# Zero rows in the first block's keys, and 32 bytes more in front of the phase pools

## The chip, the cores and the metric

One core of one Trainium2 chip runs the whole program in one launch. The metric is the device time of one execution in microseconds (us); less is better. The kernel before takes 3259.42 us, the median of three runs (3257.91 to 3260.88 us).

## The reference

Two different transformer blocks, two layers each, run one after the other on 512 tokens of width 1024, in float32. The change touches the attention of the first block and, by the places of tiles in memory, every phase of both. Cut to that:

```python
def differential_attention(q, k, v, lam_full, subln_g, lambda_init):
    s = jnp.einsum('bqhcd,bkhcd->bhcqk', qblk, kk) * Dh ** -0.5     # Dh = 64, two maps c per head
    p = jax.nn.softmax(s, axis=-1)
    a = p[:, :, 0] - lam_full * p[:, :, 1]
    return jnp.einsum('bhqk,bkhe->bqhe', a, v)

def dilated_window_attention(q, k, v, dilation, n_side):            # three dilations, 8 heads of 64
    s = jnp.einsum('brnqhd,brnkhd->brnhqk', qb, kn) * (Dh ** -0.5)
    s = jnp.where(mask, s, NEG_INF)
    e = jnp.exp(s - jnp.max(s, axis=-1, keepdims=True))
    o = jnp.einsum('brnhqk,brnkhd->brnqhd', e, vn) / den

def swiglu(h, w_gate_up, w_down):
    g, u = jnp.split(h @ w_gate_up, 2, axis=-1)
    return (jax.nn.silu(g) * u) @ w_down
```

## The kernel before, in words

**Matmuls.** Nearly every product is made of float32r matmuls on split operands: a float32 value is kept as a high part and a low part, and `mm3` (lines 309 to 313) adds high by high, and the two mixed products, in one PSUM bank: three matmuls of 128 rows, 128 weight columns and 512 (in some places 256, 360 or 384) moving columns for each step of 128 in the contraction.

**Weights.** `weights` hands them out in the order of a written plan. The SP queue loads each chunk of 1 MB, ScalarE makes the high part (line 255), VectorE the low part (line 257). The tiles `wh`, `wl` lie in the pool `stage`, the transposed activations `hTh`, `hTl` in the pool `base`. For a few chunks next to a change of phase, `spare` places `wh`, `wl` in the pool of the phase instead.

**Pools.** `setup` opens `const`, `stage`, `base` and `small`, and each phase opens its own pool behind them. `small` holds 15 tiles of 32 bytes (line 345). So the first tile of a phase pool starts 480 bytes behind the start of `small`, and an odd number of small tiles of 32 bytes shifts what follows by half a line of 64 bytes.

**Mixer of the first block** (`mixer1`). A unit (`unit`, `unit_rest`, lines 520 to 559) projects the q and k of two heads, or of one head with its two maps: for each of the two chunks c, 24 matmuls into a bank `upsum`, then the rotation: VectorE shuffles and multiplies, GpSimd (POOL) multiplies and adds. For a split unit ScalarE and VectorE then build the stack `st`: in its planes 0 and 1 the q of head e (or map e), high in its own 64 rows and low in the other 64, in planes 2 and 3 the high part of k in both halves of the rows, in plane 4 the low part of k, the rows 0 to 63 for e = 0 and 64 to 127 for e = 1. A plain unit (`d1`, `d2`) keeps q and k in float32 in two planes.

**Scores.** `score2` (lines 610 to 615) needs two matmuls: one over all 128 rows (line 613), high k against high and low q, and one over the 64 rows of e (line 615), low k against high q. Differential attention (`da_items`) does it for two maps in each of 4 blocks of 128 queries for each of 4 heads. The dilated attention (`dil_items`) does it once in each of 4 blocks for each of 8 heads, and then makes one 128-column float32 score for each of the other two dilations, over the 64 rows of its head (line 697); such a matmul shows as two passes in the trace. `weave` mixes the steps of these attentions with the units of the next heads, so that scores, transposes (lines 650, 720), value products and projections alternate on TensorE. The framework that records the program sets the final order on each engine and the waits.

**Other phases.** `merge1` makes the gates (48 matmuls a step, `gates`), the products `ab` from the tiles `oabh`, `oabl`, and the output product `acc` from `mgh`, `mgl`. `ffn1` and `ffn2` make `gu` from `hTh`, `hTl` (weights stationary) and the down product `acc` from `acth`, `actl` (weights moving). `merge2` makes its `acc` like `merge1`. At the turn of a phase, where the transposes of the next activations come in pieces, the first units (`ufirst`) and the first `gu` are made in two halves of 256 columns.

Of the kernel before, what the change touches and what calls it, by code (L numbers as in the profile page):

```python
# [224 lines left out]
class Kern:  # L225
# [118 lines left out]
    def sm(self, n, name):  # L344
        return self.small.tile([128, 8], F32, tag="sm", name=name, bufs=15)[:, :n]

# [188 lines left out]
    def unit_rest(self, c, ps, st, scale):  # L535

        nc = self.nc
        C, Sn = self.rope[:, 0, :], self.rope[:, 1, :]
        plain = st.shape[1] == 2
        sh = self.mix.tile([128, 512], F32, tag="rsh", name="rsh", bufs=2)  # L540
        z = st[:, c, :] if plain else self.mix.tile([128, 512], F32, tag="rz", name="rz", bufs=2)
        nc.vector.stream_shuffle(sh, ps, _SHUF)  # L542
        nc.vector.tensor_tensor(z, ps, C, op=OP.mult)
        nc.gpsimd.tensor_tensor(sh, sh, Sn, op=OP.mult)  # L544
        nc.gpsimd.tensor_tensor(z, z, sh, op=OP.add)
        if plain:
            return
        if c == 0:
            nc.scalar.activation(st[0:64, 0, :], z[0:64], AF.Copy, scale=scale)
            nc.scalar.activation(st[64:128, 1, :], z[64:128], AF.Copy, scale=scale)  # L550
            nc.vector.scalar_tensor_tensor(st[64:128, 0, :], z[0:64], scale, st[0:64, 0, :].bitcast(F32), op0=OP.mult, op1=OP.subtract)
            nc.vector.scalar_tensor_tensor(st[0:64, 1, :], z[64:128], scale, st[64:128, 1, :].bitcast(F32), op0=OP.mult, op1=OP.subtract)
        else:
            nc.scalar.activation(st[0:64, 2, :], z[0:64], AF.Copy)
            nc.scalar.activation(st[64:128, 3, :], z[64:128], AF.Copy)
            nc.scalar.activation(st[64:128, 2, :], z[0:64], AF.Copy)
            nc.scalar.activation(st[0:64, 3, :], z[64:128], AF.Copy)
            nc.vector.tensor_tensor(st[0:64, 4, :], z[0:64], st[0:64, 2, :].bitcast(F32), op=OP.subtract)
            nc.vector.tensor_tensor(st[64:128, 4, :], z[64:128], st[64:128, 3, :].bitcast(F32), op=OP.subtract)

    def stk(self, name):
        return self.mix.tile([128, 5, 512], F32R, tag="stk", name=name, bufs=3)

    def zst(self, name):
        return self.mix.tile([128, 2, 512], F32, tag="zst", name=name, bufs=4)

    def vfirst(self, keys, V):

        acc = [self.ps1(t, "vfirst") for t in "ssto"]
        for half, key in enumerate(keys):  # L570
            w = self.weights(key, 4, 512)
            for r in range(4):
                for k in range(4):
                    l = tuple(t[:, 4 * half + k, 128 * r:128 * r + 128] for t in self.hT)
                    self.mm3(acc[r], l, tuple(t[:, k, :] for t in w), half == 0 and k == 0, half == 1 and k == 3)
        lo = [self.mix.tile([128, 2, 512], F32R, tag="zst", name="Vl", bufs=4) for _ in range(2)]
        for r in range(4):
# [32 lines left out]
    def score2(self, out, st, e, q, k):  # L610

        mm = self.nc.tensor.matmul
        mm(out, st[:, e, q], st[:, 2 + e, k], start=True, stop=False)
        h = slice(64 * e, 64 * e + 64)
        mm(out, st[h, e, q], st[h, 4, k], start=False, stop=True)

    def da_items(self, h, st, V, Vl):
# [36 lines left out]
        def s4(rp):  # L654
# [7 lines left out]
            if rp == 1:  # L662
                nc.scalar.activation(self.oab[:, 0, h, :], O, AF.Copy)
                sq = self.mix.tile([128, 512], F32, tag="rz", name="dasq", bufs=2)
                nc.scalar.activation(sq, O, AF.Square)
# [21 lines left out]
    def dil_items(self, j, e, sts, V):  # L687
# [3 lines left out]
        def s1(r):  # L691
            ps = self.ps2("dis")
            q = slice(128 * r, 128 * r + 128)
            self.score2(ps[0], sts[0], e, q, slice(0, 512))
            own = slice(64 * e, 64 * e + 64)
            for g in (1, 2):
                nc.tensor.matmul(ps[1][:, 128 * g - 128:128 * g], sts[g][own, 0, q], sts[g][own, 1, q], start=True, stop=True)
            P = self.mix.tile([128, 1024], F32, tag="P", name="diP", bufs=3)
# [72 lines left out]
    def mixer1(self, l):  # L771
        nc, tc, aps = self.nc, self.tc, self.aps
        with tc.tile_pool(name=f"mix{l}", bufs=1, reuse_waits="tile") as mix:
# [9 lines left out]

            lam = mix.tile([128, 4, 64], F32, tag="rz", name="lam", bufs=2)
            la = aps["lam"]
# [6 lines left out]
            nc.scalar.activation(ls, ls, AF.Exp)  # L792
            self.nlam = mix.tile([128, 1], F32, name="nlam")
            nc.vector.tensor_tensor(self.nlam, ls[:, 1:2], ls[:, 0:1], op=OP.subtract)
# [13 lines left out]
            def pair_units(j):  # L808

                d = [None, self.zst("d1"), self.zst("d2")]  # L810
                Vj = []

                def first():
# [3 lines left out]
                def values():  # L817
                    Vj.append(self.newV(False))
                    yield from self.vprod([("vp", l, j, 0), ("vp", l, j, 1)], 384, Vj[0])
                return d, Vj, [self.unit(("dil", l, j, 1), d[1]), self.unit(("dil", l, j, 2), d[2]), first(), values()]  # L820

# [9 lines left out]
            d, Vj, gens = pair_units(0)  # L831
            for h, n in zip((2, 2, 3, 3), range(4)):
                fills[h].append(gens[n])
            for h in range(4):
                self.weave(chain(fills[h]), 18 * len(fills[h]), self.pipeline(self.da_items(h, sts[h], V, Vl), *STAGES_DA), 10)
            for j in range(4):
# [331 lines left out]
    def mixer2(self, l, early):  # L1168
        nc, tc, aps = self.nc, self.tc, self.aps
        with tc.tile_pool(name=f"mixb{l}", bufs=1, reuse_waits="tile") as mix:  # L1170
# [5 lines left out]
            cols = {}  # L1176
            for n, w in (("pool_scale_2", 2), ("mla_g_cq_2", 2), ("mla_g_ckv_2", 1)):
                cols[n] = mix.tile([128, w], F32, name="c_" + n)
                nc.scalar.dma_start(cols[n], aps[n + "_cols"][l])
# [430 lines left out]
```

## Time and profile before

| | us |
|---|---|
| median of three runs | 3259.42 |
| lowest, highest | 3257.91, 3260.88 |
| the profiled execution | 3256.16 |
| its span, first to last instruction | 3254.4 |
| TensorE (PE) busy in the span | 3198.2 |
| VectorE (DVE) busy | 1882.8 |
| ScalarE (ACT) busy | 1288.8 |
| GpSimd (POOL) busy | 320.2 |

The profiled execution took 1.8 us more than its span, and 3.3 us less than the median. Matmuls are pipelined: a matmul's duration holds the time in which its results drain, so the time that one costs is the distance from its start to the start of the next, and this is read from the starts in the timeline, or from the count of matmuls in a stretch in which PE is always busy.

### The profile page before, as it was taken

The numbers are of one execution on the slowest core, as the hardware profiler recorded it, in microseconds if no ns is written. First come the engines' busy times: TensorE is split into PE (matmuls) and PEld (weight loads), VectorE is DVE, ScalarE is ACT, GpSimd is POOL, SyncE is SP. The second block draws the span as 40 slices with busy tenths as digits, with TensorE's granted clock in tenths as the row PEclk, the third lists the DMA queues.
The fourth block names the chain that finished last, engine by engine and source line by source line (L and its number), as shares of the span: only waits on it lengthen the run. The fifth ranks groups of instructions, "written<-read, shape, count | busy, mean of one in ns | idle before, by whom it ended". The sixth has DMA issues, their size and how long they took to land.

```text
span 3254.4 us, 39464 instructions
## 1 busy us (share of the span) xinstructions
PE 3198.2 (98%) x15756; PEld 2613.1 (80%) x15756; DVE 1882.8 (58%) x3276; ACT 1288.8 (40%) x2268; POOL 320.2 (10%) x286
## 2 busy tenths in 40 slices
PE   8999999999999999999999999999999999999999
PEld 6788888888888788888888889668888896688887
DVE  6766666666326766666666426896332368853323
ACT  4544443433224444443422224664232246632222
POOL 1222200030001222200000000020000001200000
PEclk9999999999999999999999999999999999999999
DMA  4111124366323111124345323213223322132222
GB/s 152 46 59 59 65 100 172 132 226 223 120 102 130 37 67 59 59 99 167 137 175 199 130 92 135 67 44 136 91 91 117 121 93 72 46 128 100 94 98 84
DMA packets 62392, 351.83 MB, mean 108 GB/s; under 512 B 9276, under 2 KB 9660, under 8 KB 29184
## 3 DMA queue, kind: packets, MB, share of 16 engines
q1 hardware_dynamic: 52528, 324.59, 27.9%
q10 hardware_dynamic: 7920, 18.08, 1.7%
q0 software_dynamic: 1760, 6.65, 0.7%
q8 instruction: 123, 2.02, 0.3%
q14 instruction: 61, 0.50, 0.0%
HBM read 336.91 MB, written 12.38 MB: 107 GB/s over the span
## 4 chain that ended last, share of the span: by engine, by line
PE 92%; DVE 5%; ACT 1%; issue 0%; POOL 0%; DMA 0%; DVEq 0%; ACTq 0%; POOLq 0%
PE gu L311 10%; PE gu L313 10%; PE gu L312 10%; PE acc L311 7%; PE acc L313 7%; PE acc L312 7%; PE upsum L311 4%; PE upsum L312 3%; PE upsum L313 3%; PE gates L312 2%; PE gates L311 2%; PE gates L313 2%; DVE wl L257 2%; PE O L1425 1%; PE vacc L312 1%; PE vacc L311 1%
## 5 line engine op out<-in xcount | busy, mean ns | idle before, releaser
L257 DVE TENSOR_TENSOR wl<-wr,wh 128x1024 fp32r<-128x1024 f32 (+3 forms) x519 | 637.4, 1260 | 437.3 <-ACT wh L255 429.9
L255 ACT ACTIVATE wh<-wr 128x1024 fp32r<-128x1024 f32 (+3 forms) x520 | 492.9, 988 | 885.9 <-PE gu L312 386.9
L311 PE MATMUL gu<-hTh,wh 128*128 128x512 f32 (+1 forms) x1536 | 571.3, 372 | 0.0
L313 PE MATMUL gu<-hTh,wl 128*128 128x512 f32 (+1 forms) x1536 | 570.0, 371 | 0.0
L312 PE MATMUL gu<-hTl,wh 128*128 128x512 f32 (+1 forms) x1536 | 569.9, 371 | 0.0
L311 PEld LDWEIGHTS gu<-hTh,wh 128*128 128x128 f32 x1536 | 288.8, 188 | 54.3 <-ACT wh L255 3.4
L313 PEld LDWEIGHTS gu<-hTh,wl 128*128 128x128 f32 x1536 | 288.8, 188 | 49.9
L312 PEld LDWEIGHTS gu<-hTl,wh 128*128 128x128 f32 x1536 | 288.8, 188 | 49.8
L907 DVE TENSOR_TENSOR sg<-sg,gu 128x512 f32<-128x512 f32 x88 | 60.3, 687 | 460.0 <-PE gu L313 459.0
L311 PE MATMUL acc<-wh,acth 128*128 128x512 f32 x704 | 278.6, 396 | 0.0
L313 PE MATMUL acc<-wh,actl 128*128 128x512 f32 x704 | 277.9, 395 | 0.0
L312 PE MATMUL acc<-wl,acth 128*128 128x512 f32 x704 | 277.8, 395 | 0.0
L311 PE MATMUL upsum<-hTh,wh 128*128 128x512 f32 x448 | 188.6, 421 | 0.0
L312 PE MATMUL upsum<-hTl,wh 128*128 128x512 f32 x448 | 176.9, 395 | 0.0
L313 PE MATMUL upsum<-hTh,wl 128*128 128x512 f32 x448 | 176.4, 394 | 0.0
L544 POOL TENSOR_TENSOR rsh<-rsh,rope 128x512 f32<-128x512 f32 x64 | 87.5, 1367 | 746.7 <-DVE rsh L542 514.7
L313 PEld LDWEIGHTS acc<-wh,actl 128*128 128x128 f32 x704 | 132.0, 187 | 32.2
L312 PEld LDWEIGHTS acc<-wl,acth 128*128 128x128 f32 x704 | 132.0, 187 | 31.8
L311 PEld LDWEIGHTS acc<-wh,acth 128*128 128x128 f32 x704 | 132.0, 187 | 31.8
L906 ACT ACTIVATE sg<-gu 128x512 f32<-128x512 f32 x88 | 52.2, 598 | 262.8 <-PE gu L313 258.8
L294 DVE SCALAR_TENSOR_TENSOR m<-wr,ccols,m 128x512 f32<-128x512 f32 x168 | 126.6, 753 | 17.6 <-DMA wr<-in_wst_dram 13.2
L311 PEld LDWEIGHTS upsum<-hTh,wh 128*128 128x128 f32 x448 | 84.1, 188 | 27.6 <-issue 8.9
(419 smaller groups left out, 6076.9 us busy)
## 6 DMA issues: line engine op xcount, KB each, us to landing
wr<-in_wst_dram SPq DMA_DIRECT2D x258, 1024.0 KB, 4.8
wr<-in_wst_dram SPq DMA_DIRECT2D x28, 512.0 KB, 3.8
wr<-in_wst_dram SPq DMA_DIRECT2D x16, 768.0 KB, 4.2
xs<-x SPq DMA_DIRECT2D x12, 512.0 KB, 3.4
x<-xs SPq DMA_DIRECT2D x3, 2048.0 KB
bias<-toep SPq DMA_DIRECT2D x16, 256.0 KB, 3.7
toep<-frs POOLq DMA_DIRECT2D x12, 320.0 KB, 3.3
fu<-modrows ACTq DMA_DIRECT2D x6, 512.0 KB
```

Of the source, the lines that this page charges most:

```text
L255: self.nc.scalar.activation(hi[:, a:b], raw[:, a:b], AF.Copy)
L257: eng.tensor_tensor(lo[:, a:b], raw[:, a:b], hi[:, a:b].bitcast(F32), op=OP.subtract)
L294: nc.vector.scalar_tensor_tensor(macc, w, sc, macc, op0=OP.mult, op1=OP.add)
L311: mm(out, l[0], r[0], start=start, stop=False)
L312: mm(out, l[0], r[1], start=False, stop=False)
L313: mm(out, l[1], r[0], start=False, stop=stop)
L544: nc.gpsimd.tensor_tensor(sh, sh, Sn, op=OP.mult)
L906: nc.scalar.activation(sg[:, 0:512], ps[0], AF.Silu)
L907: nc.vector.tensor_tensor(sg[:, 512:1024], sg[:, 0:512], ps[1], op=OP.mult)
L1425: nc.tensor.matmul(O[0:64, 128 * i - 128 + a:128 * i + 128], lv, PT[:, kc, a:], start=kc == 0, stop=kc == i)
```

## The change

- The low part of k gets a plane for each e (planes 4 and 5), with zeros in the 64 rows of the other one, and the k of a plain unit gets two planes in the same way. The second matmul of `score2` and the float32 scores of the dilated attention then run over all 128 rows; what the zero rows add is zero.
- The zeros are two POOL memsets of 64 rows by 512 for every unit, ahead of the POOL work of its second chunk; the k of a plain unit is added in two POOL instructions of 64 rows instead of one of 128.
- `stk` grows to 6 planes and 4 buffers and also takes the `Vl` tiles and both plain units of a pair (`d12`); the rotation's working tile `z` alternates between one tile `rz` and a plane of `oab` that is written late (`scratch`).
- `small` has 16 tiles instead of 15; `nlam` is widened to 64 bytes and two small tiles of the second block's mixer are put into one, so that the tiles behind them stay where they were within a line.

The built programs place the operands of the float32r matmuls at these bytes of a 64-byte line:

| tiles | before | after |
|---|---|---|
| `wh`, `wl` in `stage`; `hTh`, `hTl` | 32 | 32 |
| stacks, values and `pth`, `ptl` of the mixers | 32 | 32 |
| `oabh`, `oabl`, `mgh`, `mgl`, `acth`, `actl` | 0 | 32 |
| `wh`, `wl` of the spare chunks in phase pools | 0 | 32 |

The diff, cut to its core:

```diff
@@ sm: the pool of small tiles
-        return self.small.tile([128, 8], F32, tag="sm", name=name, bufs=15)[:, :n]
+        return self.small.tile([128, 8], F32, tag="sm", name=name, bufs=16)[:, :n]
@@ unit_rest
-        plain = st.shape[1] == 2
+        plain = st.shape[1] == 3
+        halves = slice(0, 64), slice(64, 128)
         sh = self.mix.tile([128, 512], F32, tag="rsh", name="rsh", bufs=2)
-        z = st[:, c, :] if plain else self.mix.tile([128, 512], F32, tag="rz", name="rz", bufs=2)
+        z = st[:, 0, :] if plain and c == 0 else self.scratch()
         nc.vector.stream_shuffle(sh, ps, _SHUF)
         nc.vector.tensor_tensor(z, ps, C, op=OP.mult)
+        if c == 1:
+            for e in range(2):
+                other = (st[halves[1 - e], 1 + e, :] if plain else st[halves[1 - e], 4 + e, :].bitcast(F32))
+                nc.gpsimd.memset(other, 0.0)
         nc.gpsimd.tensor_tensor(sh, sh, Sn, op=OP.mult)
-        nc.gpsimd.tensor_tensor(z, z, sh, op=OP.add)
+        if plain and c == 1:
+            for e in range(2):
+                nc.gpsimd.tensor_tensor(st[halves[e], 1 + e, :], z[halves[e]], sh[halves[e]], op=OP.add)
+        else:
+            nc.gpsimd.tensor_tensor(z, z, sh, op=OP.add)
...
-            nc.vector.tensor_tensor(st[64:128, 4, :], z[64:128], st[64:128, 3, :].bitcast(F32), op=OP.subtract)
+            nc.vector.tensor_tensor(st[64:128, 5, :], z[64:128], st[64:128, 3, :].bitcast(F32), op=OP.subtract)
+    def scratch(self):
+        self.turn = 1 - self.turn
+        return self.oab[:, 1, 3, :] if self.turn else self.rz
     def stk(self, name):
-        return self.mix.tile([128, 5, 512], F32R, tag="stk", name=name, bufs=3)
+        return self.mix.tile([128, 6, 512], F32R, tag="stk", name=name, bufs=4)
     def zst(self, name):
-        return self.mix.tile([128, 2, 512], F32, tag="zst", name=name, bufs=4)
+        t = self.mix.tile([128, 6, 512], F32, tag="stk", name=name, bufs=4)
+        return t[:, 0:3, :], t[:, 3:6, :]
@@ vfirst
-        lo = [self.mix.tile([128, 2, 512], F32R, tag="zst", name="Vl", bufs=4) for _ in range(2)]
+        lo = self.mix.tile([128, 6, 512], F32R, tag="stk", name="Vl", bufs=4)
+        lo = lo[:, 0:2, :], lo[:, 2:4, :]
@@ score2
         mm(out, st[:, e, q], st[:, 2 + e, k], start=True, stop=False)
-        h = slice(64 * e, 64 * e + 64)
-        mm(out, st[h, e, q], st[h, 4, k], start=False, stop=True)
+        mm(out, st[:, e, q], st[:, 4 + e, k], start=False, stop=True)
@@ da_items, s4
-                sq = self.mix.tile([128, 512], F32, tag="rz", name="dasq", bufs=2)
+                sq = self.scratch()
@@ dil_items, s1
-            own = slice(64 * e, 64 * e + 64)
             for g in (1, 2):
-                nc.tensor.matmul(ps[1][:, 128 * g - 128:128 * g], sts[g][own, 0, q], sts[g][own, 1, q], start=True, stop=True)
+                nc.tensor.matmul(ps[1][:, 128 * g - 128:128 * g], sts[g][:, 0, q], sts[g][:, 1 + e, q], start=True, stop=True)
@@ mixer1
+            self.rz = mix.tile([128, 512], F32, name="rz")
...
-            self.nlam = mix.tile([128, 1], F32, name="nlam")
+            self.nlam = mix.tile([128, 16], F32, name="nlam")[:, 0:1]
...
-                d = [None, self.zst("d1"), self.zst("d2")]
+                d = [None, None, None]
+                def others():
+                    d[1:] = self.zst("d12")
+                    yield from self.unit(("dil", l, j, 1), d[1])
+                    yield from self.unit(("dil", l, j, 2), d[2])
@@ mixer2
+            two = mix.tile([128, 4], F32, name="c_two")
+            for n, w, at in (("pool_scale_2", 2, 0), ("mla_g_cq_2", 2, 2), ("mla_g_ckv_2", 1, None)):
+                cols[n] = mix.tile([128, w], F32, name="c_" + n) if at is None else two[:, at:at + w]
```

On POOL, in layer 0 around the first pair of plain units (in heads 2 and 3 of the differential attention; `rsh` is the shuffled copy, `d_607`, `d_608` and `d_1029` the k and q of the plain units, `d_1303` the stack of the split unit after them; waits name engines) there stood:

```order
L544 TENSOR_TENSOR rsh<-rsh,rope 128x512 [waits DVE_49]
L545 TENSOR_TENSOR d_607<-d_607,rsh 128x512 [waits DVE_49,Pool_49]
L544 TENSOR_TENSOR rsh<-rsh,rope 128x512 [waits DVE_49]
L545 TENSOR_TENSOR d_607<-d_607,rsh 128x512 [waits DVE_49,Pool_49]
L544 TENSOR_TENSOR rsh<-rsh,rope 128x512 [waits DVE_49]
L545 TENSOR_TENSOR d_608<-d_608,rsh 128x512 [waits DVE_49,Pool_49]
L544 TENSOR_TENSOR rsh<-rsh,rope 128x512 [waits DVE_49]
L545 TENSOR_TENSOR d_608<-d_608,rsh 128x512 [waits DVE_49,Pool_49]
```

and now stands:

```order
L550 TENSOR_TENSOR rsh<-rsh,rope 128x512 [waits DVE_49]
L555 TENSOR_TENSOR d_1029<-d_1029,rsh 128x512 [waits DVE_49,Pool_49]
L549 MEMSET d_1303 64x512 [waits PE_49,Pool_49]
L549 MEMSET d_1303 64x512
L550 TENSOR_TENSOR rsh<-rsh,rope 128x512 [waits DVE_49,Pool_49]
L553 TENSOR_TENSOR d_1029<-oab,rsh 64x512 [waits DVE_49,Pool_49]
L553 TENSOR_TENSOR d_1029<-oab,rsh 64x512
L550 TENSOR_TENSOR rsh<-rsh,rope 128x512 [waits DVE_49,Pool_49]
L555 TENSOR_TENSOR d_1029<-d_1029,rsh 128x512 [waits DVE_49,Pool_49]
```

The memsets of the stack `d_1303` have moved ahead of the work of the plain units, and wait for TensorE to have read the last of what lay in that buffer.

On PE, in layer 0 at the start of head 1 (`das` are the scores of the differential attention, `upsum` the projection of the next unit, `dass` the sums of squares of head 0) there stood:

```order
L613 MATMUL das_850<-da_432 128x512
L615 MATMUL das_850<-da_432 128x512
L311 MATMUL upsum<-hTh,wh_611 128x512
L312 MATMUL upsum<-hTl,wh_611 128x512
L313 MATMUL upsum<-hTh,wl_612 128x512
L311 MATMUL upsum<-hTh,wh_611 128x512
L668 MATMUL dass<-ones_85,dasq 128x1 x4
```

and now stands:

```order
L631 MATMUL das_846<-da_433 128x512
L632 MATMUL das_846<-da_433 128x512
L631 MATMUL das_847<-da_433 128x512
L632 MATMUL das_847<-da_433 128x512
L311 MATMUL upsum<-hTh,wh_609 128x512
L312 MATMUL upsum<-hTl,wh_609 128x512
L313 MATMUL upsum<-hTh,wl_610 128x512
L685 MATMUL dass<-ones_85,rz 128x1 x4
```

A block's two pairs of score matmuls, which stood apart here, now stand together; elsewhere the order of PE and DVE differs by a few places of this kind in heads 0 to 2, and in the dilated attention it is the same but for the names of tiles.

## Rows read from the trace of the kernel before

**Rows 1.** The page's busy time of TensorE: share of the span and instructions.

```profile
PE 3198.2 (98%) x15756; PEld 2613.1 (80%) x15756; DVE 1882.8 (58%) x3276; ACT 1288.8 (40%) x2268; POOL 320.2 (10%) x286
```

**Rows 2.** The page's chain that ended last, by engine.

```profile
PE 92%; DVE 5%; ACT 1%; issue 0%; POOL 0%; DMA 0%; DVEq 0%; ACTq 0%; POOLq 0%
```

**Rows 3.** Busy time by stretch: length, PE, PEld, DVE, ACT, POOL, granted clock, DMA share, GB/s.

```profile
91.00:116.00 25.00, 25.00 (x119) 18.04 (x120) 21.07 (x38) 14.46 (x30) 6.63 (x5) 1.00 0.13 43
116.00:142.00 26.00, 24.81 (x118) 18.35 (x117) 21.54 (x40) 13.06 (x27) 7.38 (x5) 1.00 0.18 59
230.00:300.00 70.00, 69.36 (x384) 58.50 (x384) 45.29 (x96) 28.75 (x54) 16.02 (x11) 1.00 0.19 68
```

**Rows 4.** What PE waited for: us in total, times, longest.

```profile
PE vacc L312 <- DVE wl L257: 5.8, 10, 0.6
...
PE dapt L650 <- DVE ptl L608: 3.0, 4, 1.2
```

**Rows 5.** Timeline of PE in layer 0, differential scores: start, duration, instruction.

```profile
67.51 0.39 PE L613 MATMUL das<-da 128*128 128x512 f32 x1
67.83 0.50 PE L615 MATMUL das<-da 64*128 64x512 f32 x1
...
69.10 0.50 PE L311 MATMUL upsum<-hTh,wh 128*128 128x512 f32 x1
69.44 0.40 PE L312 MATMUL upsum<-hTl,wh 128*128 128x512 f32 x1
```

**Rows 6.** Costliest PE groups by form, the 64-row scores: count, busy, mean.

```profile
L615 PE MATMUL das<-da 64*128 64x512 f32 x64 | 31.7, 496 | 0.0
L615 PE MATMUL dis<-d 64*128 64x512 f32 x64 | 31.7, 496 | 0.0
```

**Rows 7.** Timeline of PE in layer 0, dilated scores.

```profile
228.06 0.39 PE L613 MATMUL dis<-d 128*128 128x512 f32 x1
...
228.71 0.60 PE L697 MATMUL dis<-d 64*128 64x128 f32 x4
229.25 0.50 PE L311 MATMUL upsum<-hTh,wh 128*128 128x512 f32 x1
229.58 0.40 PE L312 MATMUL upsum<-hTl,wh 128*128 128x512 f32 x1
```

**Rows 8.** Timeline of PE, full-row float32 passes between float32r matmuls.

```profile
95.57 0.95 PE L668 MATMUL dass<-ones,dasq 128*128 128x1 f32 x8
...
96.70 0.39 PE L313 MATMUL upsum<-hTh,wl 128*128 128x512 f32 x1
```

**Rows 9.** PE alone by stretch: length, busy (matmuls), clock; gu, acc, vfirst.

```profile
2300.00:2400.00 100.00, 100.00 (x443) 1.00 0.28 103
...
885.00:965.00 80.00, 80.00 (x345) 1.00 0.28 100
...
1029.00:1047.00 18.00, 18.00 (x81) 1.00 0.01 4
```

**Rows 10.** PE groups by form whose operand moves in its line, line 311 alone.

```profile
L311 PE MATMUL acc<-wh,acth 128*128 128x512 f32 x704 | 278.6, 396 | 0.0
...
L311 PE MATMUL acc<-wh,mgh 128*128 128x512 f32 x256 | 102.0, 398 | 0.0
...
L311 PE MATMUL ab<-oabh,wh 128*128 128x512 f32 x128 | 50.7, 397 | 0.0
```

**Rows 11.** Timeline of PE: first gu of 256 columns, three starts 48 matmuls apart.

```profile
644.59 0.28 PE L311 MATMUL gu<-hTh,wh 128*128 128x256 f32 x1
...
650.33 0.28 PE L311 MATMUL gu<-hTh,wh 128*128 128x256 f32 x1
...
655.94 0.40 PE L311 MATMUL gu<-hTh,wh 128*128 128x512 f32 x1
```

**Rows 12.** POOL groups by form: adds of plain units, and a memset of 64 rows.

```profile
L545 POOL TENSOR_TENSOR d<-d,rsh 128x512 f32<-128x512 f32 x32 | 54.6, 1705 | 2.5
...
L1238 POOL MEMSET ck<- 64x1024 f32 x4 | 3.8, 947 | 839.5 <-PE acc L313 839.4
```

More of the change, by code (lines that the diff above doesn't have):

```diff
@@ L782, in mixer1 @@
             linit = 0.8 - 0.6 * math.exp(-0.3 * l)
-            lam = mix.tile([128, 4, 64], F32, tag="rz", name="lam", bufs=2)
+            self.rz = mix.tile([128, 512], F32, name="rz")
+            self.turn = 0
+            lam = mix.tile([128, 4, 64], F32, tag="rsh", name="lam", bufs=2)
             la = aps["lam"]
@@ L819, in values @@
                     yield from self.vprod([("vp", l, j, 0), ("vp", l, j, 1)], 384, Vj[0])
-                return d, Vj, [self.unit(("dil", l, j, 1), d[1]), self.unit(("dil", l, j, 2), d[2]), first(), values()]
+                return d, Vj, [others(), first(), values()]
             def chain(gs):
@@ L831, in mixer1 @@
             d, Vj, gens = pair_units(0)
-            for h, n in zip((2, 2, 3, 3), range(4)):
+            for h, n in zip((2, 3, 3), range(3)):
                 fills[h].append(gens[n])
             for h in range(4):
-                self.weave(chain(fills[h]), 18 * len(fills[h]), self.pipeline(self.da_items(h, sts[h], V, Vl), *STAGES_DA), 10)
+                self.weave(chain(fills[h]), 18 if h < 2 else 36, self.pipeline(self.da_items(h, sts[h], V, Vl), *STAGES_DA), 10)
             for j in range(4):
@@ L1176, in mixer2 @@
             cols = {}
-            for n, w in (("pool_scale_2", 2), ("mla_g_cq_2", 2), ("mla_g_ckv_2", 1)):
-                cols[n] = mix.tile([128, w], F32, name="c_" + n)
+            two = mix.tile([128, 4], F32, name="c_two")
+            for n, w, at in (("pool_scale_2", 2, 0), ("mla_g_cq_2", 2, 2), ("mla_g_ckv_2", 1, None)):
+                cols[n] = mix.tile([128, w], F32, name="c_" + n) if at is None else two[:, at:at + w]
                 nc.scalar.dma_start(cols[n], aps[n + "_cols"][l])
```

## The prediction

> **What bounds the kernel now.** I read the page's busy times first: TensorE (PE) is busy for 3198.2 of the 3254.4 us of the span [rows 1], and the chain of work that ended last runs over PE for 92% of the span [rows 2]. So a time that PE no longer needs comes off the end, as long as nothing else is late in that place. The view by stretch says where something could be: PE is never idle in head 1 of the differential attention (25.00 of 25.00 us), but VectorE (DVE) works there 21.07 us; in the dilated attention DVE has 45.29 of 70.00 us [rows 3]. The waits of PE are few: 5.8 us in ten waits of `vacc` for low parts of weights, 3.0 us in four waits of the transposes `dapt` for `ptl`, all made by DVE [rows 4]. The granted clock is 1.00 in each of these stretches, the upper level of 2.4 GHz [rows 3].
>
> A matmul's duration includes the drain, which overlaps the next, so I price by starts.
>
> **Scores of the differential attention.** The timeline shows a block's four scores and the projection behind them: from the first score at 67.51 us to the second `upsum` at 69.44 us, five matmuls take 1.93 us [rows 5]. Five matmuls of 512 columns in a run take between 5 x 226.8 and 5 x 233.2 ns (these spacings are worked out below from [rows 9]); I take 231, since a run that is broken by other work sits between. That is 1.16 us, so each block pays 0.77 us for going from 128 rows to 64 and back. Two of the 64 `das` matmuls at line 615 belong to a block [rows 6], which makes 32 blocks and 32 x 0.77 = 24.6 us. After the change all of them use 128 rows, and the cost goes.
>
> **Scores of the dilated attention.** Two score matmuls, four float32 passes over 64 rows and the next `upsum` go from 228.06 to 229.58 us: 1.52 us [rows 7]. With all rows used I price three matmuls at 231 ns, 0.69 us, and the passes from the nearest full-row float32 work: eight passes and one `upsum` take 95.57 to 96.70 us, 1.13 us, so a pass costs (1130 - 227) / 8 = 113 ns with the change of type there and back in it [rows 8]. Four make 0.45 us. The block saves 1.52 - 1.14 = 0.38 us, and there are 64 [rows 6]: 24.3 us. Scores together: 48.9 us. With 226.8 ns instead of 231 it would be 32 x 0.796 + 64 x 0.388 = 50.3 us; the other end is nothing, if what costs here is not the number of rows (third rival).
>
> The Trainium skill (TensorE: Matmul & The Clock Gate, Part 3, "What overlaps and what doesn't") says that a weight load overlaps a running matmul only when the row groups differ. By that rule all matmuls on 128 rows would wait for their weights after the change, and the scores would save nothing. The trace does not agree for full rows: `gu` needs new 128-row weights for every matmul and starts one every 226.8 ns [rows 9].
>
> **Placement.** The stretches of [rows 9] are filled with matmuls of the same shape at the same clock, and each count takes in two that were still running when the stretch began. `gu`, with both operands at byte 32 of their lines: 100.00 us / 441 = 226.8 ns. `acc` of the feed-forward, with its moving weights at 32 and its stationary activations at 0: 80.00 us / 343 = 233.2 ns. What else differs is that weights move in `acc`; in `vfirst` they move too, against `hTh` at 32, and the spacing is 18.00 us / 79 = 227.8 ns. So I put the difference down to the place in the line, between 5.4 and 6.4 ns a matmul, and take 6.0. Three lines of each group in [rows 10] make 3 x (704 + 256 + 128) = 3264 matmuls. Of these 336 use spare weights that already share the half of the line; I value them at half. That gives (2928 + 168) x 6.0 = 18.6 us, with ends at 2928 x 5.4 = 15.8 and 3264 x 6.4 = 20.9 us.
>
> There is a price in it. At a change of phase, 48 matmuls of 256 columns take 650.33 - 644.59 = 5.74 us with weights at 32, the next 48, with spare weights at 0, 655.94 - 650.33 = 5.61 us [rows 11]: shared halves are 2.7 ns slower at this width. In seven such turns 96 matmuls each move to the shared half: 672 x 2.7 ns = +1.8 us. The transposes and the rest of the second block's mixer keep their places or are not paced by them: nothing.
>
> The Trainium skill (SBUF — State Buffer, "Who interferes with whom") gives PE two independent read ports and says that PE never waits on anyone; by it, the half of a line could not matter, and this term would be 0. The 226.8 against 233.2 ns of [rows 9] speak against that, unless the spacing comes from the role of the operand.
>
> **What is late next.** In head 1 PE's 25.0 us shrink by 4 x 0.77 = 3.1 to 21.9 us, and DVE needs 21.07 us of that [rows 3]. With DVE at 96%, the scores wait now and then for `danm`, and the transposes for `ptl`. In head 2 PE already stood for 1.2 of 26 us with DVE at 21.54 us [rows 3]. For heads 0 to 2 in both layers I take 0.8 us each, +4.8 us; the ends are 0 and 6 x 3.1 = 18.6 us, all that these heads saved. In the dilated attention DVE rises from 65% to about 68%; the ten waits of `vacc` may grow by 0.1 us each, +1.0 us.
>
> **POOL.** 64 memsets at half of the 947 ns of one twice as wide make 30 us; 16 second adds at 1705 ns at most make 27 us [rows 12]. POOL had 16.02 us of work in 70 [rows 3], and the q and k of a unit are made a whole pair, or two heads, ahead: this hides them. The memsets that moved ahead in POOL's order hold eight instructions of the plain units behind them until head 2's last score is read. What those make is first read after head 3, over 40 us later, so I cost it at nothing. DVE, ACT and DMA get no more work.
>
> **Sum.** -48.9 - 18.6 + 1.8 + 4.8 + 1.0 = -59.9 us. The profiled execution took 3256.16 us, so the same execution would take 3196.3. The median of the runs is 3.3 us above it, 3259.42; carried over, I predict 3199.5 us.
>
> **The rivals.**
> 1. DVE becomes the bound in heads 0 to 2 and all that they would save is lost: 18.6 instead of 4.8 us, 3213 us. For it speaks DVE at 21.07 of the 21.9 us that PE would leave; against it, that in head 1 PE did not wait once with DVE at 84% [rows 3].
> 2. The place in the line does nothing, and `acc` is slower because of its operands' roles: the 18.6 go, and the 1.8 too, 3216 us. Against it speaks `vfirst` [rows 9]. The Trainium skill's independent ports (SBUF — State Buffer, "Who interferes with whom") lead here.
> 3. The score matmuls keep their gaps on 128 rows, because a second load of the same q, or the alternation with the float32 passes, makes them: the 48.9 go, and the wait for DVE with them, 3244 us. Against it speak [rows 8], where full rows change type and back for 113 ns a pass, and `gu` [rows 9]. The Trainium skill's rule on row groups (TensorE: Matmul & The Clock Gate, Part 3, "What overlaps and what doesn't") leads here; by `gu` it does not hold for full rows.
> 4. Slower than before: POOL becomes the end of the wait. If a pair's buffers came free only when its scores start, PE would stand at each of the eight pairs for the eight POOL instructions behind the memsets, up to 8 x 1.7 = 13.6 us, or 109 us in all: 3308 us. It is slower from 60 / 8 = 7.5 us a pair on. Against it: four buffers for what was in use two or three at a time, and units that are built a pair ahead.
>
> **How the numbers follow.** The forecast gets 0.72, the first rival 0.12, the second 0.08, the third 0.06, the fourth 0.02. The range goes from 3187 us (both gains at their upper ends, 50.3 + 20.9 - 1.8, and no wait: 3190.0, less what `upsum` may gain when scores no longer break its pace) to 3217 us, which takes in rivals 1 and 2; rivals 3 and 4 and the tails are left out. A difference of about 0.2%, 6.5 us, is what a measurement can tell from none: three of the four rivals and the forecast are faster by more; so faster 0.97, same 0.01, slower 0.02.
>
> **What would show it.** In the profile after: five matmuls from a block's first score take about 1.16 us, a dilated block 1.14; `acc` and `ab` start every 227 ns, as `gu`; the first `gu` halves all take 5.74 us for 48. PE's waits for DVE in heads 0 to 2 grow by some 5 us, and POOL's busy time by some 57 us, with no wait of PE for it. If score gaps stay above 300 ns, or `acc` at 233, that term was wrong; if heads 0 to 2 show PE idle by 3 us each, DVE took it.

## The result, and the profile after

The changed kernel takes 3216.13 us, the median of four runs (3213.48 to 3216.91), beside 3259.36 us before on the same chip: a ratio of 0.9866, 95% interval 0.9849 to 0.9883. Faster, as forecast, and just inside the range, which ends at 3217 us, but by 43.2 us where 59.9 were forecast. Two later rounds of the same kernel lie above the range: 3224.29 us (three runs, ratio 0.9889, 0.9874 to 0.9904) and 3219.31 us (four runs, 0.9876, 0.9859 to 0.9893). One more run in the first of them took 9148.72 us, at a mean granted clock of 0.333, and is left out. In the profiled executions the span fell from 3254.4 to 3214.3 us, by 40.1.

Busy times and the chain by engine on the page of after answer to [rows 1, 2]:

```profile
PE 3142.1 (98%) x15756; PEld 2623.3 (82%) x15756; DVE 1886.0 (59%) x3276; ACT 1286.7 (40%) x2268; POOL 385.5 (12%) x366
...
PE 85%; DVE 9%; ACT 3%; POOL 1%; issue 1%; DMA 1%; DVEq 0%; ACTq 0%; POOLq 0%
```

PE lost 56.1 us of busy time, the span only 40.1. PE still fills 98% of it, but the chain leaves PE more often than before (92% then): for DVE, ACT and POOL. POOL's busy time grew by 65.3 us (57 were forecast).

**What came as forecast.** The timeline of PE in after, in layer 0, a block of the differential scores and one of the dilated (to be held against [rows 5, 7]):

```profile
68.35 0.39 PE L631 MATMUL das<-da 128*128 128x512 f32 x1
68.58 0.39 PE L632 MATMUL das<-da 128*128 128x512 f32 x1
...
69.27 0.39 PE L311 MATMUL upsum<-hTh,wh 128*128 128x512 f32 x1
69.50 0.39 PE L312 MATMUL upsum<-hTl,wh 128*128 128x512 f32 x1
...
226.03 0.39 PE L631 MATMUL dis<-d 128*128 128x512 f32 x1
...
226.48 0.61 PE L713 MATMUL dis<-d 128*128 128x128 f32 x4
...
227.16 0.39 PE L312 MATMUL upsum<-hTl,wh 128*128 128x512 f32 x1
```

Four scores and an `upsum` take 69.50 - 68.35 = 1.15 us (forecast 1.16, before 1.93); the dilated block 227.16 - 226.03 = 1.13 us (forecast 1.14, before 1.52). The busy time of PE in two stretches of after, `acc` of the feed-forward and `gu` ([rows 9]):

```profile
870.00:950.00 80.00, 80.00 (x355) 1.00 0.30 106
2280.00:2380.00 100.00, 100.00 (x443) 1.00 0.27 95
```

`acc` starts every 80.00 / 353 = 226.6 ns, as `gu` does, where it was 233.2. The price of it is there too, in the timeline of the `gu` of 256 columns with spare weights, two starts 30 matmuls apart:

```profile
630.85 0.28 PE L311 MATMUL gu<-hTh,wh 128*128 128x256 f32 x1
...
634.45 0.28 PE L311 MATMUL gu<-hTh,wh 128*128 128x256 f32 x1
```

3.60 us / 30 = 120.0 ns, where these took 5.61 us / 48 = 116.9 ns with the weights in the other half [rows 11].

**Where the rest went.** PE's waits in after ([rows 4]): us in total, times, longest.

```profile
PE vacc L312 <- DVE wl L257: 7.8, 16, 0.8
PE dass L685 <- ACT rz L682: 5.4, 2, 2.7
...
PE dapt L667 <- DVE ptl L626: 3.9, 4, 1.7
...
PE dass L685 <- ACT oab L682: 2.2, 2, 1.1
```

`dass`, the sums of squares of a head, was no wait before. The timeline shows it, ACT and PE of after at the start of head 1 (heads are counted from 0), with the rows of DVE and POOL that it goes back to:

```profile
87.55 0.68 DVE L545 TENSOR_TENSOR oab<-upsum,rope 128x512 f32<-128x512 f32 x1
...
89.19 2.15 POOL L555 TENSOR_TENSOR oab<-oab,rsh 128x512 f32<-128x512 f32 x1
...
91.37 0.63 ACT L564 ACTIVATE da<-oab 64x512 fp32r<-64x512 f32 x1 [2.93 <-POOL oab L555]
...
93.86 0.57 ACT L680 ACTIVATE oab<-daO 128x512 f32<-128x512 f32 x1
94.33 0.58 ACT L682 ACTIVATE rz<-daO 128x512 f32<-128x512 f32 x1
...
91.85 0.40 PE L313 MATMUL upsum<-hTh,wl 128*128 128x512 f32 x1
94.96 1.65 PE L685 MATMUL dass<-ones,rz 128*128 128x1 f32 x8 [2.71 <-ACT rz L682]
96.48 0.77 PE L311 MATMUL upsum<-hTh,wh 128*128 128x512 f32 x1
97.05 0.63 PE L312 MATMUL upsum<-hTl,wh 128*128 128x512 f32 x1
```

and the same place on DVE, ACT and POOL before:

```profile
93.83 0.67 DVE L543 TENSOR_TENSOR rz<-upsum,rope 128x512 f32<-128x512 f32 x1
...
93.99 0.60 ACT L663 ACTIVATE oab<-daO 128x512 f32<-128x512 f32 x1 [3.85 <-PE daO L313]
94.48 0.60 ACT L665 ACTIVATE dasq<-daO 128x512 f32<-128x512 f32 x1
94.67 1.29 POOL L545 TENSOR_TENSOR rz<-rz,rsh 128x512 f32<-128x512 f32 x1 [3.05 <-ACT oab L663]
...
96.28 0.63 ACT L554 ACTIVATE da<-rz 64x512 fp32r<-64x512 f32 x1
```

Before, ACT evicted and squared O as soon as PE had made it; DVE's product for the next unit came late, at 93.83 us, and so POOL's add and ACT's copies (from 96.28 us) came behind O. Now that product is made at 87.55 us, ahead of O. The four copies of the next unit (lines 564 to 567) stand ahead of O's eviction in ACT's queue, and they wait for POOL's add. O was finished at about 90.6 us; its square comes 4 us later, and PE, for which `dass` is next, stands 2.71 us. Then the `upsum` take 0.63 us instead of 0.39: the granted clock is at its lower level of 1.2 GHz (the mean of the stretch below is 0.52). The busy view of after, heads 0 to 3 of both layers and the slow stretch (length, PE, PEld, DVE, ACT, POOL, granted clock, DMA share, GB/s):

```profile
68.00:167.00 99.00, 92.01 (x454) 75.14 (x453) 78.67 (x139) 50.07 (x104) 36.29 (x31) 0.97 0.14 48
1032.00:1129.00 97.00, 90.03 (x451) 73.38 (x450) 78.59 (x140) 50.33 (x104) 35.50 (x29) 0.98 0.17 60
...
95.00:102.00 7.00, 7.00 (x21) 5.84 (x22) 3.07 (x7) 2.78 (x8) 0.00 (x0) 0.52 0.38 150
```

Before, the four heads of a layer took 102.0 us (from the first `upsum` of head 0 to the first `vacc`, with which the value projection of the first dilated pair begins). With 16 x 0.77 = 12.3 us of score gaps gone, 89.7 should be left. After, they take 99.0 and 97.4 us: PE stands 6.9 us in each layer (1.2 before), and the half clock costs 3.4 and 1.7 us. 102.0 - 12.3 + 5.7 + 3.4 = 98.8, and 102.0 - 12.3 + 5.7 + 1.7 = 97.1: this closes the account of the heads to within 0.3 us, and 5.7 + 3.4 + 5.7 + 1.7 = 16.5 us stand where 4.8 were forecast.

### The profile page after: what moved, and what is told of

The parts are those of the page before. It is cut to its first block, busy times and chain, and to the rows that moved or that the text cites. A ratio compares the mean times of both kernels' runs of the same rounds, so it can differ in the third digit from the quotient of the medians.

```text
span 3214.3 us, 39595 instructions
## 1 busy us (share of the span) xinstructions
PE 3142.1 (98%) x15756; PEld 2623.3 (82%) x15756; DVE 1886.0 (59%) x3276; ACT 1286.7 (40%) x2268; POOL 385.5 (12%) x366
## 3 DMA queue, kind: packets, MB, share of 16 engines
q8 instruction: 123, 2.02, 0.3%
## 4 chain that ended last, share of the span: by engine, by line
PE 85%; DVE 9%; ACT 3%; POOL 1%; issue 1%; DMA 1%; DVEq 0%; ACTq 0%; POOLq 0%
PE gu L311 10%; PE gu L313 10%; PE gu L312 10%; PE acc L313 6%; PE acc L311 6%; PE acc L312 6%; DVE wl L257 3%; PE upsum L311 2%; PE upsum L313 2%; PE upsum L312 2%; PE gates L313 2%; PE gates L311 2%; PE gates L312 2%; PE O L1449 1%; PE vacc L312 1%; PE vacc L311 1%
```

## The experiments

The theory to test: the loss in the heads comes from the order on ACT (copies ahead of O), not from a lack of time on DVE; the clock falls behind PE's wait. All times below are medians of the runs, with the ratio to the kernel before on the same chip. The heads' times are read from the starts in the timeline as above; PE's waits are sums of the idle time that the timeline puts before PE's rows there; the clock's cost is half the time spent at a granted clock of 0.5.

| kernel | us | ratio, 95% interval | heads, layer 0 / 1 | PE stands | clock's cost |
|---|---|---|---|---|---|
| before | 3259.36 | 1 | 102.0 / 102.0 | 1.2 / 1.2 | 0 / 0 |
| the change | 3216.13 | 0.9866 (0.9849 to 0.9883) | 99.0 / 97.4 | 6.9 / 6.9 | 3.4 / 1.7 |
| e9_after, the change again | 3224.29 | 0.9889 (0.9874 to 0.9904) | 97.4 / 100.6 | 6.9 / 6.9 | 1.7 / 5.1 |
| e11_after, the change again | 3219.31 | 0.9876 (0.9859 to 0.9893) | 100.6 / 97.4 | 6.9 / 6.9 | 5.1 / 1.7 |
| e1_place | 3241.51 | 0.9951 (0.9939 to 0.9964) | 102.0 / 102.0 | 1.2 / 1.2 | 0 / 0 |
| e2_rows64 | 3255.98 | 0.9996 (0.9987 to 1.0005) | 109.5 / 106.3 | 3.7 / 3.8 | 5.1 / 1.7 |
| e5_scratch | 3255.02 | 0.9985 (0.9977 to 0.9994) | 107.9 / 107.8 | 3.6 / 3.6 | 3.4 / 3.4 |
| e3_order | 3214.97 | 0.9872 (0.9856 to 0.9887) | 96.7 / 96.7 | 6.5 / 6.5 | 1.7 / 1.7 |
| e4_defer | 3216.70 | 0.9876 (0.9863 to 0.9890) | 95.2 / 93.7 | 5.9 / 6.0 | 1.7 / 0 |
| e6_behind | 3207.17 | 0.9839 (0.9826 to 0.9853) | 94.4 / 92.9 | 4.2 / 4.2 | 1.7 / 0 |
| e7_behind_hp | 3206.13 | 0.9835 (0.9822 to 0.9849) | 92.1 / 92.6 | 3.7 / 3.8 | 0 / 0 |
| e10_behind_hp | 3206.69 | 0.9843 (0.9829 to 0.9856) | 93.7 / 93.7 | 3.6 / 3.7 | 1.7 / 1.7 |
| e8_add | 3205.39 | 0.9839 (0.9826 to 0.9853) | 92.1 / 93.8 | 3.6 / 3.6 | 0 / 1.7 |

The table ends at the first `vacc`. Behind it the traces of e4_defer, e6_behind, e7_behind_hp, e10_behind_hp and e8_add have another 3.4 us at half clock in each layer, and that of e3_order has 6.8 us in layer 1; the three of the change have none there. In the last four of the table the stretch from the first `vacc` to the first dilated score takes 26.0 to 26.6 us, in the change 25.5: so part of what the heads gain is given back behind them.

**e1_place: placement alone.**

```diff
-        return self.small.tile([128, 8], F32, tag="sm", name=name, bufs=15)[:, :n]
+        return self.small.tile([128, 8], F32, tag="sm", name=name, bufs=16)[:, :n]
...
-            self.nlam = mix.tile([128, 1], F32, name="nlam")
+            self.nlam = mix.tile([128, 16], F32, name="nlam")[:, 0:1]
```

(and `c_two` in the second block's mixer, as in the change.)

> Placement alone, with the mixer of the first block as before. Theory (matmuls whose moving and stationary operands lie in different halves of a 64-byte line cost 6 ns more): the down products take 3.3 us less each, the output products and the gates 4 us less together, the 256-column gu 2 us more, in all about 15 us less than before, 3244 us; the spacing of acc falls from 233 to 227 ns, and all stages of the mixer stay within 0.3 us. Rival (the spacing comes from the operands' roles, and the whole gain of the change is from the scores): 3259 us and 233 ns.

3241.51 us, 16.3 less than the 3257.85 of before beside it. The busy view of e1_place, heads and `acc`:

```profile
67.00:169.00 102.00, 100.68 (x454) 71.73 (x453) 78.26 (x140) 50.69 (x104) 26.80 (x18) 1.00 0.14 47
880.00:960.00 80.00, 80.00 (x354) 66.26 (x354) 21.04 (x23) 18.49 (x26) 0.00 (x0) 1.00 0.29 106
```

`acc` at 80.00 / 352 = 227.3 ns, the heads untouched. The forecast of placement, -18.6 + 1.8 = -16.8 us, holds, and the second rival falls.

**e2_rows64: the change with the scores over 64 rows.**

```diff
-        mm(out, st[:, e, q], st[:, 4 + e, k], start=False, stop=True)
+        h = slice(64 * e, 64 * e + 64)
+        mm(out, st[h, e, q], st[h, 4 + e, k], start=False, stop=True)
```

(and the two float32 scores of the dilated attention in the same way.)

> All of the change, but the second score matmuls and the float32 scores again over the 64 rows of their head; the zero planes, memsets, placement and the order on ACT and PE stay. Theory (PE pays for 128 to 64 to 128 rows, and the loss in head 1 comes from ACT's order, which shrinks by the 1.5 us that two blocks of scores take longer before dass): the 44 us of score gaps return, less what PE stood in head 1; 3244 to 3252 us, and PE's wait of dass is between 0.5 and 2 us in head 1. Rival (the layout made the scores faster, not the rows): within 5 us of after, 3216 us.

3255.98 us, above the expected stretch. It has the placement of e1_place and the scores of before, and so it is e1_place with the change's tiles, memsets and order: these cost 14.5 us by themselves. The rows then give 3256.0 - 3216.1 = 40 us. The view of its heads:

```profile
67.00:177.00 110.00, 106.18 (x456) 75.13 (x455) 80.58 (x143) 51.88 (x107) 36.41 (x31) 0.95 0.12 44
```

PE is the same slow PE as before in the scores, DVE has 80.58 us of work in 110, and the heads are longer than ever. A faster PE that meets a busy DVE can't be the cause of that: the waits are there without the faster scores.

**e5_scratch: of the mixer's changes, the working tile alone.** It is e1_place with

```diff
-        z = st[:, c, :] if plain else self.mix.tile([128, 512], F32, tag="rz", name="rz", bufs=2)
+        z = st[:, c, :] if plain else self.scratch()
...
-                sq = self.mix.tile([128, 512], F32, tag="rz", name="dasq", bufs=2)
+                sq = self.scratch()
```

(with `scratch` and the one tile `rz` of the change; `lam`, which is used once at the start of a layer, moves to a buffer of `rsh`, as in the change.)

> Placement of e1_place, and of the mixer's changes the scratch alone (z and dasq in turn in rz and a plane of oab); stacks, scores, memsets and the order of the units as before. On ACT the four copies of heads 0 and 1 now stand ahead of the evictions of O, as in the change. Theory (the scratch, by the order that it gives ACT and DVE, is what costs in the heads): PE waits for dass in head 1, the granted clock halves behind it, heads 0 to 3 take 12 us more than in e1_place in both layers together: 3250 to 3256 us. Rival (POOL's memsets and split adds cost it): 3240 to 3243 us, as e1_place.

3255.02 us, as the theory has it: 13.5 over e1_place by the medians, 11 by the ratios (0.9985 - 0.9951 of 3258 us), and 11.7 in the heads of the two traces; most of the 14.5. Timeline of ACT and PE in e5_scratch, and the view of its heads:

```profile
92.74 0.63 ACT L554 ACTIVATE da<-oab 64x512 fp32r<-64x512 f32 x1 [2.88 <-POOL oab L545]
...
95.23 0.57 ACT L668 ACTIVATE oab<-daO 128x512 f32<-128x512 f32 x1
...
96.33 1.05 PE L673 MATMUL dass<-ones,rz 128*128 128x1 f32 x8 [1.09 <-ACT rz L670]
...
67.00:174.00 107.00, 103.29 (x450) 73.15 (x450) 79.52 (x141) 50.95 (x105) 26.71 (x18) 0.97 0.13 45
```

No memset, no split add, no 128-row score is in this kernel, and POOL has the 26.7 us of before. The new home of `z` and `dasq` alone makes the framework put the copies ahead of O on ACT, and PE's waits and the halved clock follow. Since PE is slower here by two blocks of scores between O and `dass`, it stands 1.09 us where the change stands 2.71, a difference of 1.6 = 2 x 0.77.

**e3_order: the units of heads 0 and 1 woven more slowly.**

```diff
-                self.weave(chain(fills[h]), 18 if h < 2 else 36, self.pipeline(self.da_items(h, sts[h], V, Vl), *STAGES_DA), 10)
+                self.weave(chain(fills[h]), 12 if h < 2 else 36, self.pipeline(self.da_items(h, sts[h], V, Vl), *STAGES_DA), 10)
```

> One number: the units in heads 0 and 1 are woven more slowly, so that ACT evicts and squares O of heads 0 and 1 ahead of the four copies that wait for POOL's add. Theory (ACT's order makes PE stand 2.7 us at dass in head 1 of each layer, and the granted clock halves behind it for 6.9 and 3.4 us): 5.4 + 3.4 + 1.7 = 10.5 us less than after, 3206 us, with no half-clock stretch in the first block and no wait of dass over 1 us. Rival (DVE's work bounds heads 0 to 2): its work is the same, so within 2 us of after, 3214 to 3218 us, with the waits of PE in head 1 on DVE.

**e4_defer: `dass` made in the middle of the next head.**

```diff
-                nc.scalar.activation(sq, O, AF.Square)
-                t = self.ps1("t", "dass")
...
+                self.sums.append(h)
+            elif self.sums:
+                self.head_sums(self.sums.pop())
```

(`head_sums` squares `oab` into a free plane of it and makes the sums as before; that of head 3 comes before the first dilated pair.)

> ACT's order as in the change, but square and sums of a head (dass) are made in the middle of the next head, so that PE, and DVE's copy of the sums, don't wait for them at the start of head 1. Theory (PE's wait at dass and the halved clock behind it are the loss): 5 to 10.5 us less than after, 3206 to 3211 us; the less, the more the softmax of head 1's first scores, which stays behind the copies on ACT, becomes the next wait. Rival (DVE's work bounds heads 0 to 2): within 2 us of after.

Neither gained: 3214.97 and 3216.70 us, within what runs of the change itself differ. By the totals the theory had fallen, and the rival had the number. The heads tell more: 96.7 us in both layers of e3_order, where three executions of the change have 97.4 to 100.6, and 95.2 and 93.7 in e4_defer, which gives about 4 us a layer back between the first `vacc` and the gates, where the sums of head 3 now stand. In both, `dass` no longer holds PE, but something else does. Timeline of PE and DVE in e3_order, in head 2, and of PE in e4_defer, in head 1:

```profile
135.42 1.12 PE L667 MATMUL dapt<-ident,daP 128*128 128x128 f32 x4 [2.30 <-DVE ptl L626]
...
131.29 3.48 DVE L257 TENSOR_TENSOR wl<-wr,wh 128x1024 fp32r<-128x1024 f32 x2 [0.62 <-ACT wh L255]
```

```profile
95.51 0.50 PE L631 MATMUL das<-da 128*128 128x512 f32 x1 [2.07 <-ACT daP L652]
```

In e3_order units that are woven more slowly leave PE less to do in heads 0 and 1 (five waits of 0.7 to 1.0 us each in layer 0; the change has three of 0.4 to 0.5 there besides those of `dass`), and in head 2 transposes (`dapt`) wait 2.30 us for a `ptl` that stands behind two low parts of weights. In e4_defer the copies are still ahead, so the exponentials come late, and the scores wait for them. Both edits moved more than the one wait. What was needed was an edit aimed at the order of ACT's six instructions (four copies, eviction, square).

**e6_behind: the copies behind the eviction of O.**

```diff
-                nc.scalar.activation(self.oab[:, 0, h, :], O, AF.Copy)
+                self.evicted = nc.scalar.activation(self.oab[:, 0, h, :], O, AF.Copy)
...
+    def behind(self, c, z, st, scale):
+        with self.tc.issue_after(self.evicted.ins):
+            self.copies(c, z, st, scale)
```

(`copies` holds the copies and subtractions of lines 559 to 569 of the change; for the second chunk of a differential unit they are written behind the head that runs beside it, so DVE's two subtractions move with the copies.)

> The change, with one more edge: in heads 0 and 1 ACT's four copies of the new unit are issued behind the eviction of O; the units' speed and the place of dass stay. Theory: PE's waits at dass (2.7 + 1.1 us in each layer) and the halved clock (3.4 and 1.7 us) go: 12.7 us less than after, 3203 us. Rival (PE is ahead of a serial chain over ACT and DVE, and each wait that is taken away comes back behind the next instruction, as e3_order and e4_defer left 6 to 7.5 us of waits in a layer's heads): 3212 to 3217 us.

3207.17 us, 9 less than the change, most of the expected 12.7. Timeline of e6_behind: ACT and PE in head 1, then PE, DVE and POOL in head 2:

```profile
89.27 0.60 ACT L694 ACTIVATE oab<-daO 128x512 f32<-128x512 f32 x1 [2.22 <-PE daO L313]
...
90.24 0.62 ACT L578 ACTIVATE da<-oab 64x512 fp32r<-64x512 f32 x1
...
90.47 1.00 PE L699 MATMUL dass<-ones,rz 128*128 128x1 f32 x8
...
133.11 0.95 PE L681 MATMUL dapt<-ident,daP 128*128 128x128 f32 x4 [3.07 <-DVE ptl L640]
...
127.94 4.51 DVE L257 TENSOR_TENSOR wl<-wr,wh 128x1024 fp32r<-128x1024 f32 x2
...
127.55 3.82 POOL L556 TENSOR_TENSOR d<-oab,rsh 64x512 f32<-64x512 f32 x2
```

In head 1 the wait at `dass` is gone. Counted by the unit projected there (48 `upsum` matmuls), head 1 now takes 20.5 us instead of 26.7 and 25.1; the first three such stretches each save 2.5 to 2.7 us against before, near the 3.1 less 0.8 of the forecast. DVE works 19.3 of these 20.5 us and is no bound there. In head 2 `dapt` waits 3.07 us (1.19 before, 1.66 in the change): `ptl`, the low part of the transposes before them, is behind two low parts of weights that take 4.51 us beside POOL's two adds. The forecast had costed POOL's new work at nothing for DVE. The Trainium skill (SBUF — State Buffer, "Who interferes with whom") says that a VectorE instruction with two inputs in SBUF contends with a GpSimd instruction that reads SBUF. The traces agree: one low part takes 2.30 us beside an add of POOL (e8_add, below) and 1.23 us in the change where POOL is idle:

```profile
93.44 1.23 DVE L257 TENSOR_TENSOR wl<-wr,wh 128x1024 fp32r<-128x1024 f32 x1
```

But that it takes the second add is not shown: in e5_scratch, with the single adds of before, `dapt` waits 1.59 us in the same place, nearly as long as in the change.

**e7_behind_hp and e8_add: that wait.** e7 is e6 with

```diff
-            self.split_evict(hi, lo, pt.rearrange("p (k c) -> p k c", k=4))
+            with self.tc.high_priority():
+                self.split_evict(hi, lo, pt.rearrange("p (k c) -> p k c", k=4))
```

> As e6_behind, and the evictions of dapt (pth on ACT, ptl on DVE) get the framework's higher priority, which moves some ptl ahead of other work in DVE's queue. Theory: the remaining waits of PE in the heads for ptl and daP (3 us in each layer) shrink by a third to a half: 2 to 3 us less than e6_behind. Rival (those ptl stand behind two low parts of weights that this does not move): within 1 us of e6_behind.

and e8 is e7 with one add of 128 rows:

```diff
-        if plain and c == 1:
-            for e in range(2):
-                nc.gpsimd.tensor_tensor(st[halves[e], 1 + e, :], z[halves[e]], sh[halves[e]], op=OP.add)
-        else:
-            nc.gpsimd.tensor_tensor(z, z, sh, op=OP.add)
+        nc.gpsimd.tensor_tensor(z, z, sh, op=OP.add)
+        if plain and c == 1:
+            for e in range(2):
+                nc.scalar.activation(st[halves[e], 1 + e, :], z[halves[e]], AF.Copy)
```

> As e7_behind_hp, but the k of a plain unit is added by POOL in one instruction of 128 rows again, and ACT copies the two halves to their planes. Theory (what the change adds on POOL stretches DVE's low parts of weights beside it: in head 3 of e6_behind two of them took 4.51 us beside two adds, before 3.45 us beside one, and dapt waits behind them): the wait of dapt in head 3 falls from 2.0 to about 1 us in each layer, 2 us less in all, 3204 us. Rival (the wait is set by the order on DVE alone, or ACT's new copies come into the way): within 1 us of e7_behind_hp, 3206 us, or over it.

> The change itself once more, beside e8_add and the kernel before on one chip: 3214 to 3217 us. If e8_add is faster because of its order, it is 10 to 13 us below this run.

> e7_behind_hp once more, beside e8_add and e9_after on one chip: 3204 to 3208 us.

> The change itself a third time, since the times of e9_after lie far apart: 3214 to 3218 us if the first time of the change is the right one, 3224 us if it was a low one. In the trace, PE's wait at dass in head 1 is 2.7 us as before, and the half-clock stretches behind the waits need not be the same ones.

e7_behind_hp takes 3206.13 us, and 3206.69 in its second round (e10_behind_hp); e8_add beside that 3205.39. Timeline of e7_behind_hp, DVE and PE in head 2 (the expectation of e8_add calls it head 3):

```profile
128.06 2.30 DVE L257 TENSOR_TENSOR wl<-wr,wh 128x1024 fp32r<-128x1024 f32 x1
130.29 0.68 DVE L640 TENSOR_TENSOR ptl<-dapt,pth 128x512 fp32r<-128x512 f32 x1
...
131.02 0.66 PE L681 MATMUL dapt<-ident,daP 128*128 128x128 f32 x4 [2.02 <-DVE ptl L640]
```

and the wait of it in e8_add, both layers together, with the rows of POOL and DVE in layer 0:

```profile
PE dapt L680 <- DVE ptl L639: 4.0, 2, 2.0
```

```profile
127.94 1.62 POOL L554 TENSOR_TENSOR oab<-oab,rsh 128x512 f32<-128x512 f32 x1
...
128.34 2.30 DVE L257 TENSOR_TENSOR wl<-wr,wh 128x1024 fp32r<-128x1024 f32 x1
```

With its higher priority `ptl` now stands behind one low part instead of two, and the wait falls from 3.07 to 2.02 us; whether the total fell by the 1 us between e6 and e7 can't be told from these runs. In e8_add the wait stays at 2.0: that low part takes its 2.30 us beside one add as well. So the second add is not what is left, and the rival of e8_add holds. The two later rounds of the change gave 3224.29 (e9_after, 3215.22 to 3224.81) and 3219.31 us (e11_after), with 2.7 us of wait at `dass` in each trace; the four medians with the repaired order lie at 3205 to 3207. By the ratios the intervals of all four lie wholly below those of the two later rounds, but that of e7_behind_hp touches the interval of the change's first round and the other three overlap it a little. On one chip, side by side, the five runs of e10_behind_hp (3204.80 to 3209.52 us) all lie below the three of e9_after. So the change with the edge on ACT and the higher priority beats both kernels; the edge alone (e6_behind) was not run beside the change.

## Why the prediction was right or wrong

**Scores: right.** 1.15 and 1.13 us a block for 1.16 and 1.14. On the whole e2_rows64 against the change gives 40 us by the rows alone where 48.9 were forecast, and in the change PE stands 6.3 us more in the heads than in e2_rows64, since the faster scores meet the same late `dass`; together 46.3 us. Full rows need no gaps; the third rival is out.

**Placement: right.** -16.3 us (e1_place) for -16.8, with `acc` at 226.6 ns. The Trainium skill's independent ports of PE (SBUF — State Buffer, "Who interferes with whom") do not show in this: where the two operands start in their lines is worth 6 ns a matmul.

**"What is late next": wrong, in size and in kind.** This is the step that failed. The forecast took 4.8 us, from a DVE at 96% of its time in heads 0 to 2, with ends at 0 and 18.6. It was 16.5 us, of which 5.1 are half clock, for which the forecast had no term; and it was not DVE: e6_behind and e7_behind_hp leave DVE the same 80 to 81 us of work in the heads (79 before) and bring them to 92.1 to 94.4 us; the forecast's own sum, 102.0 - 12.3 + 2.4, is 92.1. The first rival had nearly the right time, 3213 us, from the wrong mechanism. That the first round lies inside the range is luck in part: the range reaches to 3217 us only to take in the first two rivals, of which neither holds, and the later rounds lie above it. The error has its root in the parts of the prediction on POOL and on the change: "DVE, ACT and DMA get no more work", and no price at all for the `scratch`. Both were true as amounts of work. But `scratch` lets the framework put DVE's product and POOL's add earlier, and with them ACT's copies, ahead of the eviction for which PE waits. The order on PE, DVE and POOL had been read, that on ACT not. 16.5 us is near the upper end, which was derived from the score gaps of these heads; e5_scratch, which loses 11.7 us in the heads, shows that the loss is there without any gain in the scores, so that end was no bound on it.

**Dilated attention: right but for 4.3 us.** With placement (1.4 us in each layer by e1_place) and heads taken off, the mixers and the stage behind them saved 9.5 us in each layer, 19.0 for the forecast 24.3 - 1.0 = 23.3. Waits of `vacc` for low parts grew by 7.8 - 5.8 = 2.0 us instead of 1.0, 1.4 us of waits for high parts are new, and so are 0.6 us of waits of the dilated transposes (`dipt`) for DVE; the rest, about 1 us, is not traced to a row.

**POOL: right for PE, not free for DVE.** 65.3 us more work, no wait of PE on it. An add of POOL stretches a low part beside it from 1.23 to 2.30 us, which the forecast had left out. What this added to the waits of PE is not shown: `ptl` is 1.59 us late in e5_scratch with the adds of before, 1.66 in the change, and as late in e8_add without the second add as in e7_behind_hp with it.

The sum, in the profiled executions: 40.1 us = 16.3 placement (from the medians of e1_place) + 3.0 + 4.6 heads + 19.0 dilated, less some 3 us at the start and in the second block's attention, which differ as much between two executions of e7_behind_hp.

## What to carry to other kernels

A tile that moves to another place is an edit of the order: read what stands before what on every engine, above all on the one that evicts what TensorE needs next, even where no engine gets more work. When a bound in busy time is close to a forecast, ask which queue holds the next instruction rather than how full the engine is; an edit that moves one edge (e6_behind) tells more than one that moves a whole stream (e3_order, e4_defer). And a wait of 1 to 3 us of TensorE may cost as much again in clock.

## What was not expected of the hardware

The clock's price is not fixed by the wait. Two executions of the same kernel, e7_behind_hp and e10_behind_hp, stood equally long in head 2 (2.02 and 2.01 us, in front of the same transposes). The view of the stretch behind it, e7 first:

```profile
131.00:136.00 5.00, 4.98 (x30) 4.42 (x31) 4.36 (x8) 0.60 (x1) 1.52 (x2) 1.00 0.43 151
```

```profile
133.00:136.50 3.50, 3.50 (x11) 2.85 (x11) 2.95 (x5) 0.60 (x1) 0.32 (x1) 0.51 0.26 61
```

One goes on at 1.00, the upper level of 2.4 GHz, the other at 1.2 GHz for 3.4 us. In all traces here the loss in the heads of a layer is 0, 1.7, 3.4 or 5.1 us, and the change itself had 3.4 and 1.7, 1.7 and 5.1, and 5.1 and 1.7 us in its two layers in three executions with the same waits. Over the whole execution the clock is much of why its runs lie between 3213 and 3225 us: in e9_after the run of 3215.22 us has a mean granted clock of 0.994, those of 3224.81 and 3224.29 us have 0.991 and 0.990, and by estimate 0.003 to 0.004 of 3220 us is 10 to 13 us, beside the 9 us between these runs. In e5_scratch waits of 1.09 and 0.64 us before the one-column matmuls of `dass` were followed by half clock, while 1.19 us before the transposes of head 2 cost nothing in the kernel before. What decides between these was not tested.
